# A two-layer pooling and attention trunk in fp32: one PSUM pool, the norm's matmul inside the first up product, attention's end and the last down products in another order

## The chip, the cores and the metric

The kernel runs on one core of a Trainium2 chip. The metric is device time in microseconds (us) of one execution; the time of a kernel is the median over its runs. PE is the matrix engine, DVE the vector engine, ACT the scalar engine, SP the engine whose queue issues most of the DMAs.

## The reference

One sequence of 512 tokens of width 1024 gets 16 learned tokens in front (528 in all) and goes through two residual layers. Layer 0 mixes tokens by causal pooling over windows of 2, 4, 8 and 16, layer 1 by stick-breaking attention with 16 heads of 64. A SwiGLU feed-forward of hidden width 2816 follows each, and a last RMSNorm. The 16 tokens are dropped from the output. All is float32.

```python
h = h + mixer(rmsnorm(h, g1))
h = h + (silu(rmsnorm(h, g2) @ w_gate) * (rmsnorm(h, g2) @ w_up)) @ w_down
...
z = einsum('bqhd,bkhd->bhqk', q, k) * HEAD_DIM ** -0.5
log_keep = where(mask, log_sigmoid(-z), 0.0)
later = cumsum(log_keep, axis=3, reverse=True) - log_keep
a = where(mask, exp(log_sigmoid(z) + later), 0.0)
```

## The kernel before

**Numbers.** Each fp32 operand is split into a high part (a rounding cast on ACT, `wsplit` L92 for weights) and a low part (a subtraction on DVE, L97). Each product is three matmuls, high by high, high by low, low by high (`mm3`, L102 to L108). Activations lie transposed, features on the 128 partitions and tokens along the row: `hT[c]` is chunk c of 8.

**Norms.** `Norm.chunk(c)` (L148) makes from a finished chunk the high part `uh` (ACT, L152), the low part `ul` (DVE, L153) and the square (ACT, L157), and adds squares up on DVE (L161, the last by `add_eps`, L128). `norm_bcast` (L165) sums over partitions with a matmul against ones (L173), and `rstd_of` (L132) makes the scale. The products run on the unscaled `uh` and `ul`, and the scale is multiplied in when a product is evicted.

**Feed-forward** (`ffn`, L271). The hidden width is 22 blocks f of 128. Blocks 0 to 2 are `plain` (L353): 8 chunks of gate and of up products into `pp`, evicted with the norm's scale (L364), silu (L366), product. From block 3 on a block is `strassen` (L392): 7 products of half size in place of 8, over the operands `xh`, `xl` that `operands` (L373) makes once per layer from the scaled activations, chunk pairs m and m + 4 for m = 0 to 3: DVE scales (L381) and makes differences (L387), ACT casts (L389), DVE subtracts (L390). Products go to PSUM tiles `pa`, `pb`, `pc`; ACT copies sums out (`keep`, L412), DVE and ACT form silu and the hidden block (L429 to L436), and `split_hid` splits it into `hh` and `hl` (L349, L350). The down products of a round of blocks (`ROUNDS`, four blocks each after the first two) run beside the next round's gate and up products. In layer 0 these are transposed (`down`, L295, evicted into `hT` at L304). In layer 1 they are by tokens (`down_n`, L320): t is a block of 128 tokens, e a half of the features, and `pd5_te` below is such a product of the last round. At the layer's end the last round runs over c (L462) or over t and e (L468).

**Attention.** The 16 heads are taken as 8 pairs p. `proj(p)` gives the steps of q, k and v (`half`, L503, with products `pj`). `Scores` makes the scores of a pair in three groups of key columns (`z7_832` and `z7_416` are groups of pair 7), sigmoids on ACT (L576), a scan along the row on DVE (L581) and the weights (L583). `turned` (L590) transposes a head's weights on PE (L594, L607), and ACT and DVE split them (L612 to L619); `attend` (L623) multiplies with the values into `po`; `finish` splits a pair's output into `os`. `wo(p0, p1)` (L647) gives the 8 steps of the output projection for pairs p0 to p1 − 1; `pw5_c` is chunk c of the last one, for pairs 5 to 7. The loop at L693 sets by hand what stands between: `fill` holds steps that go before, between and behind the score groups of the next pair.

**What sets the order.** Each engine works through its queue in order. A scheduler places the instructions when the program is built; `issue_after` pins one behind another. PSUM has 8 banks of 512 columns. Four phases use them in turn, each with a pool of its own: `ps0` (8 single banks) for the start, `ps1` (6 and 2) for layer 0's feed-forward, `ps2` (4 single, 2 double) for attention, `ps3` (6 and 2) for layer 1's.

**Last norm.** `square` (L738) sums squares along a row of 512 or 256 features, `store` (L744) scales a token block's two halves (L748 on ACT, L749 on DVE) and stores each with one DMA (L751).

## Time and profile before

| what | value |
|---|---|
| runs | 1058.43, 1060.87, 1235.87 us |
| median | 1060.87 us |
| the profiled execution | 1062.8 us |
| its span on the core | 1061.0 us |
| mean granted PE clock | 0.985 |
| PE, DVE, ACT busy | 96%, 81%, 52% |
| DMA | 95.73 MB, 90 GB/s |

The profile shows one execution. A timeline row has start, length, engine, line, operation, output and inputs, sizes; in brackets stands how long the engine was idle before it and what it waited for. A row of waits sums such idle time by what was waited for. A row of windows gives the busy time in a stretch. Matmul rows overlap: the distance from start to start is what one costs PE.

### The profile page before, as it was taken

The page shows a single profiled execution, that of the slowest core. Times are in us where ns is not written, and L with a number is a line of the kernel's source. Part 1 is how long each engine was busy: PE and PEld are TensorE (multiplying, and loading weights), DVE is VectorE, ACT ScalarE, POOL GpSimd, SP SyncE. Part 2 cuts the span into 40 slices and gives each one's busy share as a digit, 9 for nine tenths or more (in the row PEclk, how much of TensorE's full clock was granted, in tenths as well). Part 3 has the DMA queues.
Part 4 walks back from the last instruction along what each step waited for, and adds up shares of the span by engine and source line. Part 5 has one row for each costly group of instructions (what it writes and reads, how often), then busy time and mean ns, then how long its engine had stood idle before and what let it go on. Part 6 is the DMA issues. An engine that isn't in the chain of part 4 may idle for free.

```text
span 1061.0 us, 18586 instructions
## 1 busy us (share of the span) xinstructions
PE 1023.1 (96%) x7302; PEld 949.3 (89%) x7302; DVE 856.6 (81%) x1529; ACT 556.9 (52%) x1131; POOL 6.2 (1%) x16
## 2 busy tenths in 40 slices
PE   8998999999999999999999998989999999999997
PEld 6997999999999998998888886867899999999985
DVE  7899987888878777678888987779977877788755
ACT  7555645454444455455555454555655444455544
POOL 1000000000000010000000000000000000000000
PEclk9999999999999999999999998989999999999999
DMA  9212323333333332211111211211223223333302
GB/s 351 72 51 69 128 94 100 101 100 100 100 100 100 99 120 82 78 40 61 40 51 37 69 58 66 80 62 58 100 100 115 84 100 99 100 100 120 109 31 80
DMA packets 43112, 95.73 MB, mean 90 GB/s; under 512 B 3328, under 2 KB 20096, under 8 KB 43024
## 3 DMA queue, kind: packets, MB, share of 16 engines
q1 hardware_dynamic: 42272, 93.40, 26.2%
q8 instruction: 57, 0.93, 0.3%
q10 hardware_dynamic: 752, 1.14, 0.3%
q14 instruction: 31, 0.25, 0.1%
HBM read 92.43 MB, written 2.10 MB: 89 GB/s over the span
## 4 chain that ended last, share of the span: by engine, by line
PE 78%; DVE 17%; issue 2%; ACT 1%; DMA 1%; SPq 0%; ACTq 0%; DVEq 0%
PE pb L106 15%; PE pd L106 11%; PE pd L331 11%; PE pa L106 10%; PE pc L106 10%; PE pj L106 9%; PE pp L106 4%; DVE kp L581 2%; PE pw L106 2%; PE z L567 2%; DVE xl L390 1%; DVE a L619 1%; PE t L594 1%; DVE t L387 1%; DVE sg L583 1%
## 5 line engine op out<-in xcount | busy, mean ns | idle before, releaser
L304 DVE TENSOR_TENSOR h<-pd,h 128x264 f32<-128x264 f32 x96 | 40.9, 427 | 14.0 <-PE pd L106 14.0
L92 ACT CAST ws_3h<-rgate 128x512 fp32r<-128x512 f32 x38 | 23.6, 620 | 53.3 <-PE pb L106 47.8
L581 DVE TENSOR_TENSOR_SCAN kp<-kp,estrip 128x1344 f32<-128x1344 f32 x16 | 47.3, 2954 | 3.8 <-ACT kp L576 3.4
L92 ACT CAST ws_4h<-s 128x512 fp32r<-128x512 f32 x38 | 23.6, 621 | 46.6 <-PE pa L106 27.7
L92 ACT CAST ws_5h<-s 128x512 fp32r<-128x512 f32 x38 | 23.6, 621 | 45.8 <-PE pb L106 34.7
L433 DVE TENSOR_TENSOR u<-pb,m 128x264 f32<-128x264 f32 (+1 forms) x38 | 16.3, 428 | 38.6 <-PE pb L106 38.6
L106 PE MATMUL pa<-xl,ws_0h 128*128 128x264 f32 (+1 forms) x152 | 43.3, 285 | 3.1 <-DVE xl L390 3.0
L106 PE MATMUL pb<-xl,ws_1h 128*128 128x264 f32 (+1 forms) x152 | 43.3, 285 | 1.0 <-DVE xl L390 1.0
L106 PE MATMUL pc<-xl,ws_2h 128*128 128x264 f32 (+1 forms) x152 | 43.1, 283 | 0.9 <-DVE xl L390 0.9
L106 PE MATMUL pb<-xh,ws_1h 128*128 128x264 f32 (+1 forms) x152 | 43.6, 287 | 0.2 <-ACT xh L389 0.2
L106 PE MATMUL pa<-xh,ws_3h 128*128 128x264 f32 (+1 forms) x152 | 43.6, 287 | 0.0
L106 PE MATMUL pa<-xl,ws_3h 128*128 128x264 f32 (+1 forms) x152 | 43.5, 286 | 0.0
L106 PE MATMUL pa<-xh,ws_3l 128*128 128x264 f32 (+1 forms) x152 | 43.3, 285 | 0.0
L106 PE MATMUL pc<-xh,ws_2l 128*128 128x264 f32 (+1 forms) x152 | 43.2, 284 | 0.0
L106 PE MATMUL pa<-xh,ws_0h 128*128 128x264 f32 (+1 forms) x152 | 43.1, 284 | 0.0
L106 PE MATMUL pb<-xh,ws_6l 128*128 128x264 f32 (+1 forms) x152 | 43.0, 283 | 0.0
L106 PE MATMUL pa<-xh,ws_0l 128*128 128x264 f32 (+1 forms) x152 | 43.0, 283 | 0.0
L106 PE MATMUL pb<-xh,ws_4l 128*128 128x264 f32 (+1 forms) x152 | 43.0, 283 | 0.0
L106 PE MATMUL pc<-xl,ws_5h 128*128 128x264 f32 (+1 forms) x152 | 42.9, 283 | 0.0
L106 PE MATMUL pb<-xh,ws_1l 128*128 128x264 f32 (+1 forms) x152 | 42.9, 283 | 0.0
L106 PE MATMUL pb<-xl,ws_4h 128*128 128x264 f32 (+1 forms) x152 | 42.9, 282 | 0.0
L106 PE MATMUL pc<-xh,ws_5h 128*128 128x264 f32 (+1 forms) x152 | 42.9, 282 | 0.0
(1179 smaller groups left out, 4110.9 us busy)
## 6 DMA issues: line engine op xcount, KB each, us to landing
rgate<-in_ffn_w_gate_dram SPq DMA_DIRECT2D x44, 512.0 KB, 3.5
rup<-in_ffn_w_up_dram SPq DMA_DIRECT2D x44, 512.0 KB, 3.5
rd<-in_ffn_w_down_dram SPq DMA_DIRECT2D x42, 512.0 KB, 3.6
rq<-in_sb_w_qkv_dram SPq DMA_DIRECT2D x8, 512.0 KB, 3.5
rk<-in_sb_w_qkv_dram SPq DMA_DIRECT2D x8, 512.0 KB, 3.4
rv<-in_sb_w_qkv_dram SPq DMA_DIRECT2D x8, 512.0 KB, 3.4
rwo<-in_sb_w_o_dram SPq DMA_DIRECT2D x8, 384.0 KB, 3.0
h<-in_x_t_dram SPq DMA_DIRECT2D x8, 264.0 KB, 6.9
```

What stands on the lines that cost most here:

```text
L92: nc.scalar.copy(hi, v[:, j:j + w])
L106: last = nc.tensor.matmul(o, lhsT=w, rhs=xx[:, sl], start=start and i == 0, stop=stop and i == 2, skip_group_check=more)
L304: nc.vector.tensor_tensor(out=hv, in0=pd, in1=hv, op=ALU.add)
L331: nc.tensor.matmul(pd, lhsT=hid[j][x_][:, ts], rhs=w_[:, sl], start=r > 0 and i + j == 0, stop=j == len(hid) - 1 and i == 2, skip_group_ch ...
L387: nc.vector.tensor_tensor(out=o, in0=a, in1=b, op=ALU.subtract)
L390: nc.vector.tensor_tensor(out=xl[i][:, m, :], in0=o, in1=f32(xh[i][:, m, :]), op=ALU.subtract)
L433: tt(out=u[:, a], in0=pb, in1=m1, op=ALU.add)
L567: nc.tensor.matmul(tz[:, hd, c:c + k1 - k0], lhsT=qq[hs, i * P:(i + 1) * P], rhs=kk[hs, k0:k1], start=j == 0 and c == 0, stop=False, skip_ ...
L581: nc.vector.tensor_tensor_scan(kp[:, hd, ::-1], kp[:, hd, ::-1], estrip[:, ::-1], 1.0, op0=ALU.mult, op1=ALU.max)
L583: return nc.vector.tensor_tensor(out=sg[:, hd, 0:STRIP - 1], in0=sg[:, hd, 0:STRIP - 1], in1=kp[:, hd, 1:STRIP], op=ALU.mult).ins
L594: nc.tensor.transpose(o, sg[:, c0:c0 + n], ident)
L619: nc.vector.scalar_tensor_tensor(a0[r, i], f32(a0h[r]), lo_rows[r], p2[r, 256:384], op0=ALU.mult, op1=ALU.add)
```

## The change

**PSUM.** The four phases become one pool for the whole program: two double banks (tag `two`) and two single tags `c` and `d` of two banks each. `ps` hands out single tiles of the start and of attention in turn from these. In a Strassen block `pa` and `pb` become the halves of one two-bank tile `pab`, and the copies are made into halves of two tiles.

**Norm and operands.** The matmul of the feed-forward's norm, which stood behind the first gate product, is placed inside the first up product behind chunk `FB` = 4, and the evictions of both products stand behind it. The low halves of the weights of blocks 1 and 2 are pinned behind the norm's last sum or behind its scale. `operands` makes two chunks at once, in two passes of twice the width. `plain` and `strassen` write the silu in place.

**Attention.** `queued` pins a row of steps on PE one behind the other. Pair 7's `fill` moves: no step ahead of the first two score groups, one between, three behind. The last output projection is cut in `begun` (pairs 5 and 6) and `ended` (pair 7), and chunk c + 1 is begun before chunk c is ended.

**The end.** The last round of `down_n` is pinned in the order of t and e. The last token block is scaled and stored in pieces of 256.

```diff
+    psum = ctx.enter_context(tc.tile_pool(name="psum", bufs=1, space=bass.MemoryType.PSUM))
...
+        if tag == "any":
+            if i % 8 in (0, 1, 4, 5):
+                if i % 2 == 0:
+                    turn["tile"] = ps(name, "two", 2)
+                return turn["tile"][:, i % 2]
+            tag = "cd"[i % 2]
+        if tag == "one":
+            tag = "cd"[i % 2]
...
+                        if i == 1 and k == FB and not fst:
+                            with tc.issue_after(last):
+                                fst.extend((norm_bcast([acc], f"fb{layer}", "d"), last_rstd[0]))
+                            mark = last_bcast[0]
...
-                for m in range(4):
+                for m in (0, 2):
...
-                        xn.append(t)
-                    b11, b12, b21, b22 = [t[:, s] for t in xn for s in halves]
+                        xn.append(t)
+                    b11, b12, b21, b22 = [t[:, :, s] for t in xn for s in halves]
...
-                pa, pb, pc = [ps(f"p{i}{f}", "w")[:, :n] for i in "abc"]
+                pab = ps(f"pab{f}", "two", 2)
+                pa, pb, pc = pab[:, 0, :n], pab[:, 1, :n], ps(f"pc{f}", "c")[:, :n]
...
-                    down_n(r, t, e, prev, ws[e], "dw"[e], sl)
+                    with tc.issue_after(mark) if mark else nullcontext():
+                        mark = down_n(r, t, e, prev, ws[e], "dc"[e], sl)
...
-                fill = w[0:1], w[1:2], w[2:4]
+                fill = [], w[0:1], w[1:4]
...
-        for c, st in enumerate(wo(5, NP)):
-            st()
+        queued(lambda: begun(0))
+        for c in range(KC):
+            queued(*([lambda: begun(c + 1)] if c + 1 < KC else []), lambda: ended(c))
...
+            w = 512 if t < 3 else 256
+            cuts = [slice(o, o + w) for o in range(0, 512, w)]
```

Three places of PE's queue, before and after. A row has the line, the operation, the output, the stationary and moving operand by name and number, and the size; a wait for another engine stands in brackets.

*Layer 0's last down product (`pd5_7`) and attention's first product (`pj0_00`, over `anuh` and `anul`, the norm's parts by chunk), up to the norm's matmul (`abp0`). Before:*

```order
L106 MATMUL pd5_7_5452<-hh21_5083,wd0_5_7l0_5435 128x264
L106 MATMUL pj0_00_5504<-anuh0_5188,wq0h0_5495 128x512 [waits DVE_49,Activation_49]
L106 MATMUL pj0_00_5504<-anul0_5189,wq0h0_5495 128x512
L106 MATMUL pj0_00_5504<-anuh0_5188,wq0l0_5496 128x512
...
L106 MATMUL pj0_00_5504<-anuh7_5466,wq0h4_5499 128x512 [waits Activation_49]
L106 MATMUL pj0_00_5504<-anul7_5467,wq0h4_5499 128x512 [waits DVE_49]
L106 MATMUL pj0_00_5504<-anuh7_5466,wq0l4_5500 128x512
L173 MATMUL abp0_5529<-ansq0_5192,ones_62 128x264 [waits DVE_49]
```

*After:*

```order
L125 MATMUL pd5_7_5309<-hh21_4940,wd0_5_7l0_5292 128x264
L125 MATMUL pj0_00_5357<-anuh6_5284,wq0h4_5352 128x512 [waits Activation_49]
L125 MATMUL pj0_00_5357<-anul6_5285,wq0h4_5352 128x512 [waits DVE_49]
L125 MATMUL pj0_00_5357<-anuh6_5284,wq0l4_5353 128x512
L125 MATMUL pj0_00_5357<-anuh7_5323,wq0h4_5352 128x512 [waits Activation_49]
L125 MATMUL pj0_00_5357<-anul7_5324,wq0h4_5352 128x512 [waits DVE_49]
L125 MATMUL pj0_00_5357<-anuh7_5323,wq0l4_5353 128x512
L192 MATMUL abp0_5382<-ansq0_5049,ones_65 128x264 [waits DVE_49]
```

The 24 matmuls of `pj0_00` stood together behind the last down product; now those of chunks 0 to 5 stand among the down products, and six are left.

*The end of attention: the last output projection (`pw5_c`, over `os5` to `os7`) and the first gate product of layer 1 (`pp0`, over `f1uh`, `f1ul`). Before:*

```order
L106 MATMUL pw5_7_8528<-os7h_8359,wo5_7h0_8524 128x512
L106 MATMUL pw5_7_8528<-os7l_8360,wo5_7h0_8524 128x512
L106 MATMUL pw5_7_8528<-os7h_8359,wo5_7l0_8525 128x512
L106 MATMUL pp0_8591<-f1uh0_8380,wgate0h0_8570 128x512 [waits DVE_49,Activation_49]
L106 MATMUL pp0_8591<-f1ul0_8381,wgate0h0_8570 128x512
L106 MATMUL pp0_8591<-f1uh0_8380,wgate0l0_8571 128x512
L106 MATMUL pp0_8591<-f1uh1_8401,wgate0h0_8570 128x512 [waits Activation_49]
```

*After:*

```order
L125 MATMUL pp0_8439<-f1uh0_8244,wgate0h0_8419 128x512 [waits Activation_49]
...
L125 MATMUL pp0_8439<-f1uh1_8267,wgate0h0_8419 128x512 [waits Activation_49]
...
L125 MATMUL pp0_8439<-f1uh2_8289,wgate0h0_8419 128x512 [waits Activation_49]
L125 MATMUL pw5_7_8370<-os5h_7771,wo5_7h0_8366 128x512 [waits DVE_49]
...
L125 MATMUL pw5_7_8370<-os7h_8212,wo5_7h0_8366 128x512
L125 MATMUL pw5_7_8370<-os7l_8213,wo5_7h0_8366 128x512
L125 MATMUL pw5_7_8370<-os7h_8212,wo5_7l0_8367 128x512
L125 MATMUL pp0_8439<-f1ul2_8290,wgate0h0_8419 128x512 [waits DVE_49]
```

The gate product began behind all of `pw5`; now its first two chunks and part of the third stand ahead of the end of `pw5_7`, with `pw5_5` and `pw5_6` between them.

*The last Strassen product (`pb21`, after the change the second half of `pab21`) and the last round's down products. Before:*

```order
L106 MATMUL pb21_12400<-xh6_8560,ws21_6l0_12396 128x256
...
L331 MATMUL pd5_01_12572<-wd1_20_1h0_12546,hh20_12279 128x512 [waits Activation_49]
...
L331 MATMUL pd5_11_12616<-wd1_18_1h0_12536,hh18_11903 128x512
...
L331 MATMUL pd5_21_12660<-wd1_18_1h0_12536,hh18_11903 128x512
...
L331 MATMUL pd5_31_12704<-wd1_18_1h0_12536,hh18_11903 128x256
...
L331 MATMUL pd5_00_12554<-wd1_20_0h1_12530,hh21_12505 128x512 [waits Activation_49]
...
L331 MATMUL pd5_00_12554<-wd1_20_0h1_12530,hl21_12506 128x512 [waits DVE_49]
```

*After:*

```order
L125 MATMUL pab21_12123<-xh6_8409,ws21_6l0_12120 128x256
L351 MATMUL pd5_00_12274<-wd1_20_0h1_12250,hh21_12225 128x512 [waits Activation_49]
L351 MATMUL pd5_00_12274<-wd1_20_0h1_12250,hl21_12226 128x512 [waits DVE_49]
L351 MATMUL pd5_00_12274<-wd1_20_0l1_12251,hh21_12225 128x512
L351 MATMUL pd5_01_12292<-wd1_18_1h0_12256,hh18_11635 128x512
L351 MATMUL pd5_01_12292<-wd1_18_1h0_12256,hl18_11636 128x512
```

Before, 28 matmuls on blocks 18 to 20 stood between the last Strassen matmul and the first use of `hh21`; now that use follows at once.

More of the change, by code (lines that the diff above doesn't have):

```diff
@@ L31 @@
 PLAIN = 3
+FB = 4
 NW = 8
@@ L61, in blk, with ps_pair @@
         return main.tile([P, n], dt, tag="blk", name=name, bufs=NBLK)
-    @contextmanager
-    def phase(name, **bufs):
-        with tc.tile_pool(name=name, bufs=1, space=bass.MemoryType.PSUM) as pool:
-            psum["pool"], psum["bufs"] = pool, bufs
-            yield
-    def ps(name, tag, banks=1):
-        shape = [P, 512] if banks == 1 else [P, banks, 512]
-        return psum["pool"].tile(shape, F32, tag=tag, name=name, bufs=psum["bufs"][tag])
+    psum = ctx.enter_context(tc.tile_pool(name="psum", bufs=1, space=bass.MemoryType.PSUM))
+    turn = {"one": 0, "any": 0, "pair": 0}
+    def ps(name, tag, banks=1):
+        i = turn.get(tag, 0)
+        turn[tag] = i + 1
+        if tag == "any":
[6 more added lines that the diff above has]
+            tag = "cd"[i % 2]
+        shape = [P, 512] if banks == 1 else [P, banks, 512]
+        return psum.tile(shape, F32, tag=tag, name=name, bufs=2)
+    def ps_pair(name):
+        i = turn["pair"]
+        turn["pair"] = i + 1
+        if i % 3 == 2:
+            return [ps(f"{name}{j}", "c") for j in range(2)]
+        pt = ps(name, "two", 2)
+        return [pt[:, 0], pt[:, 1]]
     def wraw(src, name):
@@ L126, in add_eps @@
     def add_eps(out, sq, acc):
[L128 to L130 removed]
+        return nc.vector.scalar_tensor_tensor(out, sq, D * EPS / P, acc, op0=ALU.add, op1=ALU.add).ins
+    last_rstd, last_bcast = [], []
     def rstd_of(parts, r, t):
@@ L172, in norm_bcast @@
             for i, acc in enumerate(accs):
-                nc.tensor.matmul(p, lhsT=ones, rhs=acc[:, o:o + h], start=i == 0, stop=i == len(accs) - 1)
+                last_bcast[:] = [nc.tensor.matmul(p, lhsT=ones, rhs=acc[:, o:o + h], start=i == 0,
+                                                  stop=i == len(accs) - 1).ins]
             parts.append((p, slice(o, o + h)))
@@ L179, in trunk @@
     norm = Norm(16, "f0")
-    with tc.tile_pool(name="start", bufs=1) as sp, phase("ps0", one=8):
+    with tc.tile_pool(name="start", bufs=1) as sp:
         nc.scalar.activation(sp.tile([P, 1], F32, name="table"), ones[:, 0:1], AF.Abs_reciprocal_sqrt)
@@ L330, in down_n @@
                 for i, (x_, w_) in enumerate(((0, wh), (1, wh), (0, wl))):
-                    nc.tensor.matmul(pd, lhsT=hid[j][x_][:, ts], rhs=w_[:, sl], start=r > 0 and i + j == 0,
-                                     stop=j == len(hid) - 1 and i == 2, skip_group_check=r == 0)
+                    last = nc.tensor.matmul(pd, lhsT=hid[j][x_][:, ts], rhs=w_[:, sl], start=r > 0 and i + j == 0,
+                                            stop=j == len(hid) - 1 and i == 2, skip_group_check=r == 0)
             hv = hn[4 * e + t][:, sl]
@@ L388, in operands @@
                     for i, o in enumerate((b11, t2, t1, b21, t3, b22, t4)):
-                        nc.scalar.copy(xh[i][:, m, :], o)
-                        nc.vector.tensor_tensor(out=xl[i][:, m, :], in0=o, in1=f32(xh[i][:, m, :]), op=ALU.subtract)
+                        hi, lo = xh[i][:, m:m + 2, :], xl[i][:, m:m + 2, :]
+                        nc.scalar.copy(hi, o)
+                        nc.vector.tensor_tensor(out=lo, in0=o, in1=f32(hi), op=ALU.subtract)
             def strassen(f):
@@ L480, in before_attention @@
         return norms[0].chunk
-    with phase("ps1", w=6, d=2):
-        ffn(0, 16, norm, before_attention)
-    with tc.tile_pool(name="att", bufs=1) as ap, phase("ps2", one=4, two=2):
+    ffn(0, 16, norm, before_attention)
+    with tc.tile_pool(name="att", bufs=1) as ap:
         uh, ul, acc = norms[0].uh, norms[0].ul, norms[0].acc
@@ L588, in both, with queue, queued @@
                     self.weights(1)
+        pos = []
+        def queue():
+            return tc.issue_after(pos[0]) if pos else nullcontext()
+        def queued(*steps):
+            for st in steps:
+                with queue():
+                    pos[:] = [st()]
         def turned(p, hd, sg):
@@ L668, in begin @@
             sc = Scores(p, got["q"], got["k"])
-            mark = None
-            for st in before:
-                mark = st()
-            with tc.issue_after(mark) if mark else nullcontext():
-                sc.group(0)
-                mark = sc.group(1)
-            for st in between:
-                with tc.issue_after(mark):
-                    mark = st()
-            with tc.issue_after(mark):
-                sc.group(2)
+            queued(*before, lambda: (sc.group(0), sc.group(1))[1], *between, lambda: sc.group(2))
             sc.both()
@@ L686, in trunk @@
         sg = begin(0, got, [], steps[3:4])
-        steps[4]()
+        queued(steps[4])
         values()
         nxt, steps, values = proj(1)
-        for st in steps[:3]:
-            st()
+        queued(*steps[:3])
         early, w = wo(0, 2), wo(2, 5)
```

131 lines of the change are left out of this document (76 added, 55 removed).

## The prediction

> **What bounds the kernel now.** I read the page's busy shares and the shares of the chain first.
>
> ```profile
> PE 1023.1 (96%) x7302; PEld 949.3 (89%) x7302; DVE 856.6 (81%) x1529; ACT 556.9 (52%) x1131; POOL 6.2 (1%) x16
> PE 78%; DVE 17%; issue 2%; ACT 1%; DMA 1%; SPq 0%; ACTq 0%; DVEq 0%
> ```
>
> TensorE is busy for 1023.1 of 1061.0 us; VectorE at 81% is second, and it takes over for 17% of the chain. Where it does so is not in an average, so I cut the span into stages. Each row below is a stretch, its length, then busy time with count of PE, weight loads, DVE, ACT and POOL, then granted clock, DMA share and GB/s.
>
> ```profile
> 76.00:98.00 22.00, 17.55 (x113) 15.43 (x112) 22.00 (x56) 11.31 (x29) 0.00 (x0) 0.92 0.14 51
> 98.00:390.00 292.00, 292.00 (x2400) 292.00 (x2399) 237.45 (x447) 148.15 (x301) 3.27 (x10) 1.00 0.32 105
> 700.00:760.00 60.00, 57.42 (x303) 48.81 (x302) 53.05 (x109) 33.87 (x72) 0.00 (x0) 0.96 0.18 62
> 760.00:1030.00 270.00, 270.00 (x1888) 251.91 (x1888) 211.21 (x375) 138.82 (x284) 0.00 (x0) 1.00 0.30 98
> ```
>
> In the two long feed-forward stretches PE has no gap in 562 us, and nothing that only reorders work can gain there. From 76 to 98 DVE has no gap and PE idles 4.45 us: the activations' Strassen operands are made there, and from 700 to 760 for the second layer. What a reordering can win is in the waits of PE (from whom, total, times, longest):
>
> ```profile
> PE pp L106 <- DVE h L660: 4.1, 1, 4.1
> PE t L594 <- DVE sg L583: 3.6, 1, 3.6
> PE pa L106 <- DVE xl L390: 3.0, 3, 2.1
> PE pb L106 <- DVE xl L390: 1.0, 1, 1.0
> PE pc L106 <- DVE xl L390: 0.9, 1, 0.9
> PE z L567 <- DVE a161l L616: 0.6, 1, 0.6
> ```
>
> **A second price stands behind a wait: the granted clock.** Here the stretches are cut where the clock records change; after the busy time of PE with its count comes the clock.
>
> ```profile
> 38.86:42.27 3.41, 3.21 (x14) 0.50 0.43 156
> ...
> 86.65:90.06 3.41, 3.16 (x13) 0.50 0.00 0
> ...
> 421.16:424.57 3.41, 1.79 (x14) 1.00 0.13 35
> 424.57:427.98 3.41, 3.41 (x23) 0.50 0.31 124
> ...
> 653.26:656.67 3.41, 0.60 (x4) 1.00 0.00 0
> 656.67:663.50 6.83, 6.05 (x20) 0.50 0.22 77
> 690.81:694.22 3.41, 0.20 (x1) 1.00 0.45 150
> 694.22:701.05 6.83, 5.89 (x14) 0.50 0.22 79
> 738.59:742.00 3.41, 2.16 (x12) 1.00 0.00 0
> 742.01:745.42 3.41, 3.41 (x23) 1.00 0.02 5
> 745.42:748.83 3.41, 2.35 (x12) 1.00 0.00 0
> 748.84:752.25 3.41, 3.41 (x17) 0.50 0.43 154
> ```
>
> A stretch of 3.41 us in which PE was busy for 1.79 or less is followed by half rate for 3.41 or 6.83 us; after 2.16 it stayed full once, after 2.35 it fell once. Half rate is real time:
>
> ```profile
> 661.32 0.63 PE L106 MATMUL pw<-os3l,wo_4h 128*128 128x512 f32 x1
> 661.75 0.63 PE L106 MATMUL pw<-os3h,wo_4l 128*128 128x512 f32 x1
> ...
> 1041.40 0.39 PE L331 MATMUL pd<-wd_0h,hh 128*128 128x512 f32 x1
> 1041.63 0.40 PE L331 MATMUL pd<-wd_1h,hh 128*128 128x512 f32 x1
> ```
>
> 512 columns start 0.43 us apart in the first pair, 0.23 in the second. The six half-rate rows hold 25.1 us of PE work, so about 12.6 us is lost to them. I charge 1.7 us (half of 3.41) for each new stretch, times the chance that a wait falls so that it empties one.
>
> The Trainium skill, "TensorE: Matmul & The Clock Gate", Part 1, has the same window (3413 ns, free-running) but says that the clock turns cold after at least one idle window. The trace agrees on the window and not on the condition: the fall at 424.57 follows a window that was busy for 1.79 us. That condition as the Trainium skill states it would lead to the third rival's time.
>
> **The change, place by place** (+ is slower). Times are worked out on the profiled execution, 1062.8 us, which is 1.9 above the median.
>
> *Feed-forward steady state: 0.* One pair of PSUM banks now serves two products, so the copy of m1 holds the first product of `pb` in the same tile, and the silu of `pa` waits for `pb`'s end. In PE's order products of `pc` and down products worth at least 2 us stand between in the steady state; a copy out of PSUM takes about 0.4 (the 264-wide eviction below is 0.43). Price if that cover is gone: the second rival.
>
> *Start of layer 0: +0.5 (−1.5 to +2.5).* The norm's matmul stands inside the first up product, some 1.2 us earlier. The operands come in two passes of two chunks instead of four, so the first product gets its first operand's two chunks together, and its third and fourth wait for a whole second pass.
>
> ```profile
> L304 DVE TENSOR_TENSOR h<-pd,h 128x264 f32<-128x264 f32 x96 | 40.9, 427 | 14.0 <-PE pd L106 14.0
> ```
> ```profile
> 1037.40 0.69 DVE L350 TENSOR_TENSOR hl<-u,hh 128x512 fp32r<-128x512 f32 x1
> ```
>
> Two 264-wide DVE operations take 0.85, one twice as wide 0.69: between nothing and 0.16 is saved on each of 22 pairs; since operations overlap by some 0.07 to 0.1 at their ends I take 0.07, or 1.6. Walking the queues, PE stalls about 9 us in place of the 4.9 of the three `xl` rows, but reaches this place 2.4 earlier: 9 − 4.9 − 2.4 − 1.6 ≈ 0; I leave 0.5 for the later operands.
>
> *Layer 0's end into attention: +3.2 (+1.6 to +4).*
>
> ```profile
> 408.83 0.47 PE L106 MATMUL pj<-anuh,wq0h 128*128 128x512 f32 x1 [0.69 <-ACT wq1h L92]
> ...
> 414.47 1.05 PE L173 MATMUL abp<-ansq,ones 128*128 128x264 f32 x4
> ```
> ```profile
> 411.18 0.70 DVE L128 SCALAR_TENSOR_TENSOR ansq<-ansq,ansq 128x528 f32<-128x528 f32 x1
> ```
>
> The last down product ends at 408.83 − 0.69 = 408.14. The chain from it (eviction of h7, high and low half, square, sum) ends at 411.88, 3.74 later. Before, 24 matmuls of `pj0_00` covered all of it, up to the norm's matmul at 414.47. Now 18 of them stand among the down products, each behind its chunk, and 6 are left: 6 × 0.23 = 1.4. So 2.35 stands bare where 0.69 did: +1.7. One more down product waits for the eviction before it, +0.3. The stall is broken by single matmuls; I give it 7 chances in 10 of a half-rate stretch, +1.2.
>
> *Pairs 0 to 4: 0; pairs 5 and 6: +0.3 (0 to +0.9)*, since two `wo` steps now stand before the next transposes, whose inputs are ready, and so delay ACT's and DVE's work behind these.
>
> *Pair 7: −0.9 (−2.5 to +0.5).* `fill` gives no step ahead of the first two score groups; 9 matmuls (2.1 us) leave the place before `z7_832`. That group's wait for `a161l` grows from 0.6 by 2.1. In return the third group stands ahead of three steps, 27 matmuls (6.2), and `po61` (1.5) covers the scan and what follows it:
>
> ```profile
> 651.83 2.96 DVE L581 TENSOR_TENSOR_SCAN kp<-kp,estrip 128x1344 f32<-128x1344 f32 x1 [1.64 <-ACT kp L576]
> ...
> 655.76 1.55 DVE L583 TENSOR_TENSOR sg<-sg,kp 128x1343 f32<-128x1343 f32 x1
> ```
>
> 2.96 + 1.55 plus a wait is under 7.7, so the 3.6 us gap goes, with its half-rate stretch (6.05/2 = 3.0). Evictions now queue behind the second scan, about +2.0 in three waits. 2.1 − 3.6 + 2.0 − 3.0 = −2.5; the new 2.7 us wait costs a stretch of its own, +1.7 at most: −0.9.
>
> *Attention's end into layer 1: −3.9 (−6.5 to −1).* Matmuls of pair 7's last products and of the first gate product alternate, each behind its chunk. The 4.15 idle and 5.89/2 = 2.95 of half rate go: −7.1. But DVE then makes the operands in about 38 us of its own, before and after, from the norm's scale to the last `xl` (from 700 to 760 it is busy for 53.05 of 60). The scale comes only 5.7 earlier, and PE arrives with more to wait for: +2.4, and +0.8 as half a chance of a further stretch.
>
> *The tail: +4.3 (+1.5 to +7).* The last products are pinned token by token.
>
> ```profile
> 1030.90 0.42 ACT L432 ACTIVATE sg<-g 128x256 f32<-128x256 f32 x1
> ...
> 1035.18 0.28 PE L106 MATMUL pb<-xh,ws_6l 128*128 128x256 f32 x1
> ...
> 1036.75 0.62 ACT L349 CAST hh<-u 128x512 fp32r<-128x512 f32 x1 [0.70 <-DVE u L436]
> ```
>
> From 1035.30, when PE was free, to 1041.40, when the first product took `hh` of block 21, PE had 28 matmuls on other blocks; `hh` was ready at 1037.37, `hl` at 1038.09. Now the first product behind the last Strassen matmul needs `hh`. The silu (0.42) reads the same PSUM tile and stands ahead: `hh` at 1037.8, a bare wait of 2.5; one matmul; `hl` at 1038.5, another 0.5. In front of that the last Strassen product waits for the copy of `m67`, about 1.0. A half-rate stretch after it is nearly certain, +1.7. At the very end there is a gain:
>
> ```profile
> 1052.78 0.28 PE L331 MATMUL pd<-wd_1l,hh 128*128 128x256 f32 x1
> ...
> 1056.57 0.72 ACT L748 ACTIVATE hn<-fss 128x512 f32<-128x512 f32 x1 [0.47 <-DVE fss L139]
> ```
>
> The last scaled piece is ready 4.23 after the last matmul's end. The third and the fourth block of tokens no longer share DVE's queue there, and the pieces are 256 wide (0.42 for 0.72, but two of them): 2.85 by the same operations, −1.4. It has 2 stores more, whose issue lies beside other work. 1.0 + 3.0 + 1.7 − 1.4 = 4.3.
>
> Weight loads and their DMAs move with their steps on SP's queue; at 51 to 105 GB/s in these stretches I charge nothing, and up to 0.5 if a moved one were late, inside the ranges.
>
> **Sum.** 0.5 + 3.2 + 0.3 − 0.9 − 3.9 + 4.3 = +3.5: 1066.3 for an execution like the profiled one, 1060.87 + 3.5 = **1064.4** for the median. The places' ends do not all come together; the forecast's own range is 1055 to 1075.
>
> **Rivals.**
> *Only the gaps close.* The waits of 4.1, 3.6 and 0.7 go with the half-rate stretches at 656.67 and 694.22 (6.0), the stores give 1.4, and what I count as bare is covered by work that I placed wrongly: −15.8, **1045**. For it: these gaps are the three that the edits sit on. Against: PE's queue is in order, and in the tail nothing stands between.
> *The shared PSUM tile holds PE in the steady state.* Each of 38 Strassen blocks waits for m1's copy, 0.4 and a handoff of 0.2: +23, **1084**, slower than before. It decides when less than 0.6 us of other products stands between `pa`'s last and `pb`'s first; I count at least 2.
> *Waits without a drop of the clock.* If only a nearly empty window (0.60 and 0.20 of 3.41 in the rows) were followed by half rate, the new waits, broken or under 3 us, would cost themselves alone: 1.2 + 1.7 + 0.8 + 1.7 = 5.4 less, **1059**. Against it stand the falls at 424.57 and 748.84. The Trainium skill's condition ("TensorE: Matmul & The Clock Gate", Part 1) would give this time.
> *More opens.* Tail, operands of both layers and layer 0's end at the top of their ranges: +3.5 + 2.7 + 2.0 + 2.9 + 0.8 = +12, **1073**.
>
> **Chances.** Forecast 0.55, gaps alone 0.18, shared tile 0.05, no drop 0.12, more opens 0.10. The range of 1048 to 1075 leaves out the shared tile and a good half of the first rival. A measurement of this kernel can tell 2%, that is 1039.7 or 1082.1: faster 0.05 (the far side of the first rival), slower 0.04, same 0.91.
>
> **What would show it.** Right: no wait of PE at the first `pp` product behind attention nor at pair 7's transposes; new waits at `abp`, at `z7_832` and of 2.5 us at the first `pd5_00` product with `hh` of block 21, each followed by clock 0.50; the last store's source ready about 2.9 us after the last matmul. Wrong: PE under 292 in 292 in the steady state; no wait in the tail; or clock 1.00 behind waits of 2 us and more.

## The result: 1073.41 us, slower by 1.3%

| what | before | after |
|---|---|---|
| median | 1060.77 us (4 runs) | 1073.41 us (4 runs, 1072.82 to 1075.66) |
| ratio, 95% interval | | 1.0131 [1.0106, 1.0155] |
| the profiled execution | 1062.8 us | 1073.62 us |
| its span | 1061.0 us | 1071.5 us |
| mean granted PE clock | 0.985 | 0.979 |

One run of the kernel before, 1235.87 us, was disturbed and is left out of the ratio. The changed kernel is 12.6 us slower by the medians and 10.5 us by the two spans. The forecast was 1064.4 with a range to 1075. The time lies in the range, but it is the time of the rival "more opens", 1073, and not that of the forecast.

**The page after**, busy shares:

```profile
PE 1029.0 (96%) x7302; PEld 951.3 (89%) x7302; DVE 858.5 (80%) x1486; ACT 551.3 (51%) x1104; POOL 7.2 (1%) x16
```

The number of matmuls is the same. PE is busy 5.9 us longer with them, most of it half rate: the half-rate rows below hold 34.2 us of PE work, those of the kernel before 25.1, and half of the difference is 4.5. The other 4.6 of the 10.5 us is idle time. These are PE's longest waits (from whom, total, times, longest):

```profile
PE pab L125 <- DVE xl L425: 4.8, 2, 2.5
PE pool L268 <- DVE pl L275: 3.3, 2, 2.7
PE pd L351 <- ACT hh L370: 3.1, 1, 3.1
PE z L601 <- DVE a161l L662: 2.7, 1, 2.7
PE pd L351 <- DVE hl L371: 2.6, 1, 2.6
```

The waits of 4.1 (`pp` behind attention's end) and 3.6 (pair 7's transposes) are gone. In their place stand waits for `a161l` and for `hh` of block 21, and smaller ones for `anul` at layer 0's end and for `mb` in the tail (rows below), at the places that the prediction named. The wait for `pl`, in the start's pooling stage, and the one for `hl`, at 739.43 among layer 1's operands, it did not name.

**A long stretch and layer 1's operands after** (stretch, length, busy time with count of PE, weight loads, DVE, ACT, POOL; clock, DMA share, GB/s):

```profile
98.00:390.00 292.00, 292.00 (x2398) 291.81 (x2396) 235.80 (x446) 141.70 (x297) 0.00 (x0) 1.00 0.31 104
706.00:710.28 4.28, 4.28 (x20) 3.54 (x19) 0.05 (x1) 2.58 (x4) 0.00 (x0) 1.00 0.68 235
710.28:750.94 40.66, 34.50 (x150) 27.82 (x150) 40.59 (x67) 20.76 (x35) 0.00 (x0) 0.87 0.19 63
```

In the steady state PE has no gap, before and after, so the shared PSUM tile holds nothing up. In the last row DVE is the engine without a gap, and PE idles for 6 us; in the row above it, DVE stands idle for 4.23 of 4.28 us. That pair of rows carries the miss of the prediction at attention's end.

**The clock after** (stretch, length, PE busy with count, clock, DMA share, GB/s), each half-rate stretch behind the window ahead of it:

```profile
17.02:20.43 3.41, 0.70 (x6) 1.00 1.06 386
20.43:23.84 3.41, 3.41 (x18) 0.50 1.04 412
78.45:81.86 3.41, 1.58 (x11) 1.00 0.21 85
81.87:92.10 10.23, 7.26 (x28) 0.50 0.12 43
416.37:419.78 3.41, 1.91 (x6) 1.00 0.03 12
419.79:423.19 3.40, 3.40 (x12) 0.50 0.30 94
645.06:648.47 3.41, 0.73 (x7) 1.00 0.28 113
648.48:655.29 6.81, 6.81 (x31) 0.50 0.01 2
737.22:740.63 3.41, 1.19 (x4) 1.00 0.00 0
740.64:750.87 10.23, 6.93 (x23) 0.50 0.14 40
1037.60:1041.00 3.40, 0.75 (x7) 1.00 0.00 0
1041.01:1047.83 6.82, 6.39 (x14) 0.50 0.01 2
```

Each of the waits above has half rate behind it or around it, and four of the six stretches last 6.8 or 10.2 us rather than 3.41.

**Where the time went.** The table follows PE through its queue by the start of the same matmul, or of the matmul with the same number, in both profiled executions.

| point | before | after | difference | added since |
|---|---|---|---|---|
| first gate product of block 0, layer 0 | 39.06 | 40.35 | +1.3 | +1.3 |
| 1500th matmul, mid feed-forward of layer 0 | 204.97 | 207.81 | +2.8 | +1.5 |
| first key product of pair 2 | 456.12 | 461.40 | +5.3 | +2.5 |
| last key product of pair 7 | 614.04 | 619.41 | +5.4 | +0.1 |
| last projection's first matmul (`os5`) | 674.12 | 680.45 | +6.3 | +1.0 |
| first up product of block 1, layer 1 | 715.53 | 715.63 | +0.1 | −6.2 |
| 6300th matmul, mid feed-forward of layer 1 | 903.11 | 907.36 | +4.3 | +4.2 |
| last matmul | 1052.78 | 1064.65 | +11.9 | +7.6 |
| end of the span | 1061.0 | 1071.5 | +10.5 | −1.4 |

Each column is one execution, and which windows half rate falls into differs between executions of the same instructions. The run `before_fill` below has those of the kernel before up to pair 7, but reaches the same first gate product later, with the same wait in front of it (the kernel before, then `before_fill`):

```profile
39.06 0.78 PE L106 MATMUL pp<-f0uh,wgate0h 128*128 128x264 f32 x2 [2.19 <-DVE h L266]
```
```profile
40.77 0.48 PE L106 MATMUL pp<-f0uh,wgate0h 128*128 128x264 f32 x2 [2.19 <-DVE h L266]
```

So a difference at one place of up to 1.7 us, the price of one stretch of 3.41, is not shown to come from the change.

### The profile page after: what moved, and what is told of

Read it like the earlier page. It is cut to its first block, busy times and chain, and to the rows that moved or that the text cites. A ratio compares the mean times of both kernels' runs of the same rounds, so it can differ in the third digit from the quotient of the medians.

```text
span 1071.5 us, 18530 instructions
## 1 busy us (share of the span) xinstructions
PE 1029.0 (96%) x7302; PEld 951.3 (89%) x7302; DVE 858.5 (80%) x1486; ACT 551.3 (51%) x1104; POOL 7.2 (1%) x16
## 4 chain that ended last, share of the span: by engine, by line
PE 77%; DVE 17%; ACT 3%; issue 2%; DMA 1%; SPq 0%; DVEq 0%; ACTq 0%
PE pab L125 25%; PE pd L351 12%; PE pd L125 11%; PE pc L125 10%; PE pj L125 9%; DVE kp L615 2%; PE z L601 2%; PE pw L125 2%; PE pp L125 1%; DVE a L665 1%; DVE xl L425 1%; DVE sg L617 1%; PE mix L125 1%; DVE xn L415 1%; DVE of L682 1%
## 5 line engine op out<-in xcount | busy, mean ns | idle before, releaser
L125 PE MATMUL pab<-xl,ws_0h 128*128 128x264 f32 (+1 forms) x152 | 43.7, 288 | 4.8 <-DVE xl L425 4.8
L125 PE MATMUL pc<-xh,ws_2h 128*128 128x264 f32 (+1 forms) x152 | 43.5, 286 | 1.1 <-DVE u L397 1.1
L125 PE MATMUL pab<-xh,ws_0h 128*128 128x264 f32 (+1 forms) x152 | 43.4, 285 | 1.0 <-ACT xh L424 1.0
L125 PE MATMUL pab<-xh,ws_6h 128*128 128x264 f32 (+1 forms) x152 | 43.0, 283 | 0.9 <-ACT mb L456 0.9
L125 PE MATMUL pab<-xh,ws_0l 128*128 128x264 f32 (+1 forms) x152 | 43.7, 287 | 0.0
L125 PE MATMUL pab<-xh,ws_6l 128*128 128x264 f32 (+1 forms) x152 | 43.1, 283 | 0.0
L125 PE MATMUL pab<-xh,ws_4l 128*128 128x264 f32 (+1 forms) x152 | 43.0, 283 | 0.0
L125 PE MATMUL pab<-xl,ws_1h 128*128 128x264 f32 (+1 forms) x152 | 43.0, 283 | 0.0
L125 PE MATMUL pab<-xh,ws_1h 128*128 128x264 f32 (+1 forms) x152 | 43.0, 283 | 0.0
L125 PE MATMUL pab<-xl,ws_3h 128*128 128x264 f32 (+1 forms) x152 | 43.0, 283 | 0.0
```

What stands on the lines that cost most here:

```text
L125: last = nc.tensor.matmul(o, lhsT=w, rhs=xx[:, sl], start=start and i == 0, stop=stop and i == 2, skip_group_check=more)
```

## The experiments

The theory at this point: the loss sits in three places where the change bares a chain on DVE and ACT (layer 0's end, pair 7, the tail), each with half rate behind it, and in layer 1's operands, where PE's earlier arrival meets a scale that comes later than forecast. The rivals were that the pool's banks and not the pins bare the tail, and that the clock alone, not the chains, makes the loss. Four runs changed the kernels as given. All ratios are to the kernel before, timed in the same rounds (its medians there: 1059.54 to 1060.76); changes that leave part of the loss in place are compared by their medians.

**The tail without its pins** (`tail_free`).

```diff
-                    with tc.issue_after(mark) if mark else nullcontext():
-                        mark = down_n(r, t, e, prev, ws[e], "dc"[e], sl)
+                    down_n(r, t, e, prev, ws[e], "dc"[e], sl)
```

> The changed kernel with one thing undone: the last round's down products are no longer pinned by tokens. Theory 1 (the pins took the cover away): the cover of about 6 us comes back, the wait of 3.1 us at hh of block 21 and the half rate behind it (6.83 us, 3.4 lost) go, about -6, near 1067. Theory 2 (the cover is lost by the number of free PSUM banks: one pool leaves four banks to these products, and their work on blocks 18 to 20 is put ahead of the last Strassen product): 2 matmuls stand in the gap, the wait stays at about 2.6 and the clock still falls; only the copy's wait of 0.9 and the second wait at hl go, -1 to -2, near 1072.

Measured: 1069.82, ratio 1.0097 [1.0083, 1.0111], 3.6 better than the changed kernel: neither 6 nor 1 to 2. PE's timeline behind the last Strassen product (start, length, then the operation; a wait in brackets), and the clock there:

```profile
1043.78 0.63 PE L351 MATMUL pd<-wd_1l,hh 128*128 128x512 f32 x2
1047.03 0.50 PE L351 MATMUL pd<-wd_0h,hh 128*128 128x512 f32 x1 [2.62 <-ACT hh L370]
```

```profile
1042.21:1045.62 3.41, 2.20 (x16) 1.00 0.00 0
1045.62:1049.03 3.41, 2.00 (x9) 1.00 0.00 0
```

Without the pins the scheduler again puts work on blocks 18 to 20 early, but ahead of the last Strassen product: only four bank-sized tiles are left for the last products in the one pool, so it starts four pairs, and two matmuls stand in the gap. The wait stays at 2.62. What is gained is the wait for `m67` and the half rate: the idle time is split over two windows, each busy for 2.00 or more, and the clock did not fall. So the pins alone do not bare the tail; the scheduler's order in the one pool does it without them.

**The tail with cover put in by hand** (`tail_cover`). The products over blocks 18 to 20 of the first two token blocks are pinned behind the last Strassen product; block 21's follow in the order of t and e.

```diff
+            for t, e in ((0, 0), (0, 1), (1, 0), (1, 1)):
+                with tc.issue_after(mark or lastmm[0]) if t + e else nullcontext():
+                    mark, half[t, e] = down_n(r, t, e, prev, ws[e], "dc"[e], part=slice(0, 3))
```

> The changed kernel with the last down products still pinned, but in another order: the products of blocks 18 to 20 of the first four (token, half) pairs stand behind the last Strassen product, ahead of the first use of block 21. Same work, 19 matmuls (4.4 us) in the gap. Both theories of the tail: the wait at hh of 3.1 us, the copy's 0.9 and the half rate behind (3.4) go: -6 to -7, near 1067. If the tail's loss were something else than the bare chain (the pieces of the stores, the shared tile), it would stay above 1071.

Measured: 1067.13, ratio 1.0071 [1.0055, 1.0087], 6.3 better than the changed kernel. The timeline, up to the first product with block 21:

```profile
1038.63 0.39 PE L351 MATMUL pd<-wd_1l,hh 128*128 128x512 f32 x1
...
1043.03 0.39 PE L351 MATMUL pd<-wd_0h,hh 128*128 128x512 f32 x1
```

```profile
750.50:1061.00 310.50, 306.61 (x2114) 1.00 0.30 95
```

PE goes on for 4.4 us on the other blocks, no row of that stretch has a wait, and the clock is 1.00 from there to the end. The last matmul comes 7.8 us earlier than in the changed kernel. The stall in the tail with what follows it cost these 6.3 us, shown by taking it away. The same four tiles serve here, so it is the order and not the number of tiles that bares the chain.

**The tail's wait filled with work nobody reads** (`tail_fill`): 13 matmuls more, into an unread PSUM tile, in the place of the wait for `hh`. The chain to `hh` stays as it is.

```diff
+                    spare = ps("spare", "two", 2)[:, 0]
+                    with tc.issue_after(lastmm[0]):
+                        for _ in range(NFILL):
+                            last = nc.tensor.matmul(spare, lhsT=hid[0][0][:, ts], rhs=w[0][0][:, sl], start=True,
+                                                    stop=True)
```

> The changed kernel with 13 extra matmuls (3.0 us; their sums go to a PSUM bank that nobody reads) between the last Strassen product and the first use of block 21's hh. The chain behind the wait is not shorter. Theory: the clock falls because PE stood idle for most of a 3.41 us window, so with PE kept busy it stays at 1.00 from 1041 to 1048: -3.4, near 1070. Rival: the clock falls for another reason (time, load, the end of a phase): no change, 1073, and 0.50 still in those windows.

Measured: 1071.82, ratio 1.0117 [1.0104, 1.0131]: 1.6 better by the medians, with intervals that overlap. In the trace:

```profile
1039.04 3.15 PE L356 MATMUL spare<-wd_0h,hh 128*128 128x512 f32 x13
1042.28 0.50 PE L361 MATMUL pd<-wd_0h,hh 128*128 128x512 f32 x1
```

```profile
1038.91:1042.33 3.42, 3.33 (x17) 1.00 0.00 0
```

The clock stays at 1.00, in the next window too. The way from the last `ws_4l` product to the span's end is 33.4 us against 36.0: 2.6 of the tail's loss is clock, and the rest bare chain. The clock's part is read from the trace; the medians alone do not resolve it.

**The same in the kernel before** (`before_fill`): 14 spare matmuls in front of pair 7's transposes and 16 behind the last projection, where it had 3.6 and 4.1 us of waiting and two half-rate stretches.

```diff
+            if p == NP - 1:
+                spare = ps("spare", "two", 2)[:, 0]
+                with tc.issue_after(lastpo[0]):
+                    for _ in range(14):
+                        nc.tensor.matmul(spare, lhsT=osp[0][0][:, 0:P], rhs=osp[0][0], start=True, stop=True)
```

> The kernel before with 14 extra matmuls in the 3.6 us gap ahead of pair 7's transposes and 16 in the 4.15 us gap at the end of attention (their sums go to PSUM that nobody reads). Theory: the two half-rate stretches of 6.83 us behind these gaps go, 6.05/2 + 5.89/2 = 6.0 less, near 1055; the waits themselves stay. Rival (the clock falls for another reason): 1061 or, if the extra work delays the next product, above.

Measured: 1058.22, ratio 0.9993 [0.9985, 1.0002], where the price of half the busy time gives 6. Both stretches are at full clock:

```profile
658.28:661.69 3.41, 3.41 (x17) 1.00 0.00 0
...
695.83:699.24 3.41, 3.41 (x16) 1.00 0.15 61
```

By the trace the stage at attention's end is 2.8 shorter, close to the priced 2.95, but the one at pair 7 only 1.1, against 3.0. There PE, now faster, waits for DVE instead:

```profile
664.79 0.38 PE L633 MATMUL po<-a270l,vv 128*128 128x256 f32 x1 [0.25 <-DVE a270l L616]
666.16 0.50 PE L633 MATMUL po<-a,vv 128*128 128x512 f32 x1 [0.98 <-DVE a L619]
```

The kernel before has no such waits there. Two things follow: half rate costs its full half only where PE sets the end; and even the 3.9 us that the trace shows is not in the medians (−1.3). The profiled execution of the kernel before is longer than most: it lies 1.9 above its median, and its mean clock of 0.985 is below that of all 17 runs timed beside `before_fill` (0.986 to 0.990). So a usual run has less half rate to lose. Its stretch at 424.57, for one, is absent in `before_fill`, where nothing was edited up to there.

The next four stand on `tail_cover` and undo or change one part each, so their base is 1067.13.

**The norm's matmul of layer 1 behind the first chunk** (`c_fb`), in place of chunk 4; layer 0 is left.

```diff
-FB = 4
+FB = (4, 0)
```

> tail_cover with one more thing moved: in layer 1 the norm's matmul stands behind chunk 0 of the first up product instead of chunk 4 (layer 0 keeps 4). In the changed kernel's trace the sum of squares is ready at 703.6, the matmul starts at 707.6, and DVE stands idle for 4.2 us until the scale. Theory (DVE bounds the stretch from the scale to the last operand, about 40 us): the scale comes 3 us earlier, PE's waits at the operands shrink by as much, -3, near 1064. Rival (PE bounds the stretch, or the table load and the evictions behind set it): 0 to -1, 1066 to 1067.

Measured: 1064.10, ratio 1.0041 [1.0025, 1.0057], −3.0. DVE's timeline of the changed kernel, from the last square's sum to the scale, then PE's row for the norm's matmul, and DVE's in this run:

```profile
702.93 0.70 DVE L147 SCALAR_TENSOR_TENSOR f1sq<-f1sq,f1sq 128x528 f32<-128x528 f32 x1
...
710.28 0.71 DVE L155 TENSOR_TENSOR fb1t<-fb1r 128x528 f32<-128x528 f32 x1 [4.24 <-ACT fb1r L154]
```
```profile
707.60 1.05 PE L192 MATMUL fb1p<-f1sq,ones 128*128 128x264 f32 x4
```
```profile
701.12 0.70 DVE L147 SCALAR_TENSOR_TENSOR f1sq<-f1sq,f1sq 128x528 f32<-128x528 f32 x1
...
705.69 0.71 DVE L155 TENSOR_TENSOR fb1t<-fb1r 128x528 f32<-128x528 f32 x1 [1.46 <-ACT fb1r L154]
```

In the changed kernel the sum of squares is ready at 703.63 and the norm's matmul, behind four chunks of the up product, starts at 707.60; DVE idles for 4.24. In this run sum to scale takes 4.6 us instead of 7.4. By the traces the operands' stage gets 2.2 shorter. Another 1.5 comes from pair 7, where the half-rate stretch is 3.41 instead of 6.83 long; nothing of the edit is there, so that part is not the edit's.

**Operands in four passes again, in both layers** (`c_ops`).

```diff
-                for m in (0, 2):
+                for m in range(4):
```

> tail_cover with the operands made in four passes of one chunk again. Theory 1 (two passes make PE wait: first products need the second pass early): PE's waits at both layers' operands fall, -1.5 in layer 0 and -2 in layer 1, near 1063.5. Theory 2 (DVE bounds these stretches, and the twice as wide operations save it time): 22 more DVE operations per layer at 0.07 each, +1.6 per layer at most, 1067 to 1070.

Measured: 1065.96, ratio 1.0052 [1.0036, 1.0068], −1.2 with overlapping intervals. By stages it is two results: up to the twelfth Strassen block of layer 0 +2.1, in layer 1's feed-forward −2.1. In layer 0 the waits for `xl` (the longest 2.2 us between 70 and 125 us in the changed kernel) go and another takes their place; PE's longest there in this run:

```profile
PE pd L125 <- DVE h L324: 4.6, 4, 2.2
```

The evictions of layer 0's first down products stand in DVE's queue among the operands. Neither expectation holds in both layers: four passes gain nothing in layer 0 and are better in layer 1. That they cost 2.1 in layer 0 is not shown. Here the half-rate stretch is 13.65 us long, 6.83 in the base; `c_wo` below, with two passes as in the base, has one of 13.65 too and is 1.6 later than the base at the 1500th matmul.

**Attention's first product whole behind the last down product** (`c_pj`).

```diff
-        for st in steps[:3]:
+        with tc.issue_after(lastdown[0]):
+            steps[0]()
+        for st in steps[1:3]:
             st()
```

> tail_cover with attention's first product pinned behind layer 0's last down product again, 24 matmuls in one piece. Theory: the waits of 0.6 and 0.9 at the last two chunks and of 0.5 between the down products go, -2.0, and so does the half-rate stretch behind them where the window falls so, up to -1.7: -2 to -3.5, near 1064.5. Rival (the loss there comes from the pool, not from the order): no change.

Measured: 1062.52, ratio 1.0023 [1.0011, 1.0036], −4.6, more than expected. PE's rows of the changed kernel, then PE's window of this run around the same place:

```profile
417.34 0.50 PE L125 MATMUL pj<-anul,wq0h 128*128 128x512 f32 x1 [0.64 <-DVE anul L172]
...
419.24 0.50 PE L125 MATMUL pj<-anul,wq0h 128*128 128x512 f32 x1 [0.86 <-DVE anul L172]
```
```profile
405.00:430.00 25.00, 23.37 (x168) 1.00 0.26 86
```

The two waits and the half rate at 419.79 are gone. The stage is 3.6 shorter by the trace, and pair 7, where nothing was edited, again 1.5, with a half-rate stretch of 3.41. The profiled execution, at 1059.78, is among the fastest of this kernel's 12 runs (1059.71 to 1064.60), so the trace shows more gain (spans 1063.8 and 1057.8) than the medians do.

**Pair 7's steps between the score groups as before** (`c_p7`).

```diff
-                fill = [], w[0:1], w[1:4]
+                fill = w[0:1], w[1:2], w[2:4]
```

> tail_cover with pair 7's fill as before: one projection step ahead of the first score groups, one between, two behind. Theory: the wait of 2.7 us for a161l falls to 0.6 and the half-rate stretch behind it goes (6.83 us, 3.4); the cover of the scan shrinks by 9 matmuls to 5.7 us, so about 1 us of wait comes back ahead of the transposes: -2 to -4, near 1064. Rival (the wait only moves: the 3.6 us gap of the kernel before comes back whole, with its half rate): 0 to +1.

Measured: 1063.52, ratio 1.0036 [1.0023, 1.0049], −3.6; the stage is 4.05 shorter. The waits at the third score group and at the transposes, after this edit; in the changed kernel the first was 2.67, and the second had gone:

```profile
647.71 0.50 PE L607 MATMUL z<-qk_1h,qk_0h 64*128 64x512 f32 x2 [0.57 <-DVE a161l L668]
...
660.02 0.74 PE L645 MATMUL t<-consts,sg 128*128 128x128 f32 x5 [0.83 <-DVE sg L623]
```
```profile
640.00:676.00 36.00, 32.94 (x199) 1.00 0.22 72
```

The clock is 1.00 throughout. The gap at the transposes is only 0.83 with the old `fill` too (3.6 in the kernel before), so moving `fill` was not needed to close it. What differs in PE's queue is the order that `queued` pins: it has 9 projection matmuls ahead of the third score group and 18 behind it, where the scheduler of the kernel before had put 21 ahead and 6 behind.

**All of it together** (`best`): `tail_cover`, `c_fb`, `c_pj` and `c_p7`, with operands in two passes in layer 0 (`full`) and four in layer 1.

```diff
+                two = full
+                for m in (0, 2) if two else range(4):
```

> tail_cover with what the single runs showed put together: the norm's matmul of layer 1 behind chunk 0, attention's first product in one piece, pair 7's fill as before, operands in two passes in layer 0 and in four in layer 1. If the places are independent, the stage differences add: 1067.1 - 2.2 (scale earlier) - 3.6 (first product) - 4.1 (pair 7) - 2.1 (four passes in layer 1) = 1055, about 4 under the kernel before. If the four passes and the earlier scale give the same time twice (both shorten the wait for DVE's operands), -2 less: 1057.

Measured: 1054.36, ratio 0.9949 [0.9936, 0.9961]: 5.5 faster than the kernel before and 19 faster than the change as made. What is left of PE's longest waits, beside the start's for `pl` (3.4 in two):

```profile
PE pd L345 <- ACT hn L357: 2.8, 1, 2.8
```

In layer 1 the down products of the first round wait for an eviction (0.8 in the changed kernel), probably since PE arrives earlier.

**Weight sums of one block per layer on GpSimd** (`best_pool`), to relieve DVE where it sets the end.

```diff
-                        nc.vector.tensor_tensor(out=o, in0=a, in1=b, op=op)
+                        (nc.gpsimd if f == PLAIN else nc.vector).tensor_tensor(out=o, in0=a, in1=b, op=op)
```

> The kernel best, with the four weight sums of the first Strassen block of each layer on POOL instead of DVE (4 x 0.68 us of DVE less in each layer's stretch of operands; POOL is idle there). Theory (DVE bounds these stretches): PE's waits shrink by up to 2.7 in each layer, -3 to -5 against best. Rival (POOL is so slow, or shares so much with DVE, that the sums come late and hold the first Strassen products): 0 or slower than best.

Measured: 1066.60, ratio 1.0058 [1.0044, 1.0072]: 12.2 slower than `best`. First one of GpSimd's four sums in a layer, for both layers (count, then busy total and mean ns), then DVE's low halves of two weights while it ran, then the same two in `best`:

```profile
L442 POOL TENSOR_TENSOR s<-rgate,rup 128x512 f32<-128x512 f32 x2 | 3.5, 1740 | 0.0
```
```profile
58.55 3.51 DVE L116 TENSOR_TENSOR wup2l<-rup,wup2h 128x512 fp32r<-128x512 f32 x2
```
```profile
57.64 1.29 DVE L116 TENSOR_TENSOR wup2l<-rup,wup2h 128x512 fp32r<-128x512 f32 x2
...
58.85 0.68 DVE L442 TENSOR_TENSOR s<-rup 128x512 f32<-128x512 f32 x1
```

This sum takes 1.74 us on GpSimd, one on DVE 0.68, and DVE's own two operations take 3.51 in place of 1.29 meanwhile. The scheduler also moved work at layer 0's end, with a new half-rate stretch there, so not all of the 12 us comes from the slower sums and DVE operations.

**The last projection in whole chunks again** (`c_wo` on `tail_cover`, `best_wo` on `best`), to see whether the interleaving `begun`/`ended` closed the wait of 4.1 us, or the one pool.

```diff
-        queued(lambda: begun(0))
-        for c in range(KC):
-            queued(*([lambda: begun(c + 1)] if c + 1 < KC else []), lambda: ended(c))
+        wos = wo(5, NP)
+        queued(lambda: (wos[0](), norms[1].chunk(0))[0])
+        for c in range(1, KC):
+            queued(lambda: (wos[c](), norms[1].chunk(c))[0])
```

> tail_cover with attention's last projection in whole chunks again, one after the other as before the change, in the one PSUM pool. Theory 1 (the 4.15 us wait was the border between two PSUM pools: the first gate product waited for the last eviction): without a border the product starts at once behind the last projection and keeps pace with the norm's halves, PE loses at most 1.5, and the stretch behind is bound by DVE from a scale that comes at nearly the same time: 0 to +1.5, 1067 to 1068.5. Theory 2 (the interleaving of the chunks made the gain): the wait of about 4 us and a half-rate stretch come back ahead of the gate product, +4 to +7, 1071 or more.

> The kernel best with attention's last projection in whole chunks again. Theory 1 (the border between pools made the wait): +0 to +1.5, 1054.4 to 1056. Theory 2 (the interleaving made the gain, and only shows where the scale is not late for another reason): +3 to +5, 1057.5 to 1059.5.

Measured: 1067.21, ratio 1.0063 [1.0051, 1.0075], beside 1067.13 for `tail_cover`; and 1055.63, 0.9959 [0.9946, 0.9972], beside 1054.36 for `best`. No difference that can be told. The stage up to the first up product of block 1 is 1.4 longer, and layer 1's operands give 0.95 of it back. The 4.1 us did not return with the whole chunks, so the interleaving did not close it. By elimination it belonged to the border between the pools, where the first product of the next phase took a bank of attention's; no run interleaves with two pools.

## Why the prediction was right in range and wrong in its sum

Point by point, as the sum had it; the sizes are those of the table by places.

**Steady state, forecast 0: right.** PE is busy 292.00 of 292.00.

**Start and operands of layer 0, forecast +0.5: +2.8.** The table puts +1.3 of this before the first gate product, in the pooling stage, which the prediction did not price. There the tiles come in turn from another set of banks, and one matmul waits 2.7 us for `pl`, while the 2.19 in front of the first gate product is gone. But the +1.3 can't be put down to the change: the start has one half-rate stretch of 3.41 in each of three traces, at 38.86 before, behind that product, and at 20.43 after and 19.98 in `before_fill`, ahead of it. Beside `before_fill` the changed kernel reaches the product 0.4 earlier and the 1500th matmul (205.60 there) 2.2 later, so by these traces the loss lies at the operands. Between 70 and 125 PE is idle for 5.6 us, less than the 9 that "Walking the queues, PE stalls about 9 us" gave, but the half-rate stretch there lasts 10.23 us (one of 3.41 before), which was not foreseen. The four-pass run gets nothing of it back, so the two passes are not shown to be the cause.

**Layer 0's end, forecast +3.2: +2.5, right in mechanism, the size in part by luck.** Waits for the eviction's chain, then half rate; `c_pj` takes both away and 3.6 with them. The kernel before had a stretch of its own near there in its profiled execution, at 424.57; beside `before_fill`, which has none, the stage is 3.9 longer.

**Pairs 5 and 6, forecast +0.3: +0.1, right.**

**Pair 7, forecast −0.9: +1.0, wrong sign.** (Its terms add up to −0.8.) The wait for `a161l` was forecast as 0.6 + 2.1 and is 2.67:

```profile
647.90 0.50 PE L601 MATMUL z<-qk_1h,qk_0h 64*128 64x512 f32 x2 [2.67 <-DVE a161l L662]
```

The step that failed is "the new 2.7 us wait costs a stretch of its own, +1.7 at most": the stretch is 6.81 us long with 6.81 of work in it, 3.4 of loss; behind the same wait it was 3.41 long in `c_fb` and `c_pj`. And the 3.0 credited for the old half rate was too much, since `before_fill` gets only 1.1 from it: DVE's `a` is next.

**Attention's end into layer 1, forecast −3.9: −2.1.** The gap closes as forecast: −6.2 up to the up product of block 1, against −7.1. The step that failed is "The scale comes only 5.7 earlier". The operations that end in the scale `fb1r` follow DVE's row at 710.28 in the changed kernel and at 708.29 before:

```profile
708.29 0.71 DVE L136 TENSOR_TENSOR fb1t<-fb1r 128x528 f32<-128x528 f32 x1 [2.30 <-ACT fb1r L135]
```

Counted from the last projection's first matmul (680.45 and 674.12) that is 29.8 us and 34.2, so the scale comes 4.3 earlier. I had moved the norm's matmul forward by the time that PE gained, and not looked at what stands ahead of it in the new order: four chunks of the up product. DVE, which sets the end from there on, stood idle for 4.24 us ahead of it, 2.30 before. So of the 6.2 that PE gained, 4.2 were returned in front of the operands, where it waits and runs at half rate for 10.23 us (3.41 before); the term of +0.8 for a further stretch was too small as well. `c_fb` and `c_ops` recover 2.2 and 2.1 there.

**The tail, forecast +4.3: +7.6 at the last matmul, −1.4 behind it, +6.3 in all.** The chain is the one described, link by link: the wait for `m67` 0.86 (forecast 1.0), for `hh` 3.09 (2.5), and the last store's −1.4 (−1.4). PE's and ACT's rows:

```profile
1036.67 0.39 PE L125 MATMUL pab<-xh,ws_6h 128*128 128x256 f32 x1 [0.86 <-ACT mb L456]
...
1041.44 0.80 PE L351 MATMUL pd<-wd_0h,hh 128*128 128x512 f32 x1 [3.09 <-ACT hh L370]
```
```profile
1038.33 0.62 ACT L111 CAST wd_1h<-rd 128x512 fp32r<-128x512 f32 x1 [1.71 <-PE pab L125]
1038.86 0.38 ACT L462 ACTIVATE sg<-pab 128x256 f32<-128x256 f32 x1
```

Two terms were mis-sized. ACT casts a weight between the products' end and the silu, which puts the silu at 1038.86; its 0.62 is the size by which `hh` is later than priced. And "a half-rate stretch after it is nearly certain, +1.7" was a stretch of 3.41; it lasted 6.82 with 6.39 of work, 3.2 of loss (2.6 by `tail_fill`). The prediction blamed the pins; `tail_free` shows that the cover is gone without them too, by the scheduler's order in the one pool, and `tail_cover` that pins in another order bring it back.

**The clock.** The common error is the price of one stretch. The falls came after windows that were busy for 0.70, 0.73, 0.75, 1.19, 1.58 and 1.91 of 3.41 us, so the rival "waits without a drop" fell with them; the windows of 2.00 and 2.20 in `tail_free` kept full clock. The Trainium skill ("TensorE: Matmul & The Clock Gate", Part 1) asks for at least one idle window; the row of 1.91 shows a fall where PE worked for over half of it. Busy time is not all of it, though: in `before_fill` the window from 37.05 to 40.46, busy for 1.53, was followed by full clock. What was wrong was the length, taken as 3.41 although the prediction's own rows have two of 6.83 behind the waits of 3.6 and 4.1: at layer 0's operands, pair 7, layer 1's operands and in the tail it was 6.8 to 10.2.

**The range** held only because it took in the rival that opens four places at their worst. That its 1073 is the measured time is luck: layer 0's end and attention's end stayed inside their ranges, and pair 7, which it leaves out, gave 1.9 of the miss. What the places have in common is one cause, a chain on DVE or ACT laid bare with half rate behind it, so their terms do not average out as independent ones would.

Open remain what stretches the half rate at layer 0's operands, and how much of a half-rate stretch's length is chance. The pins on the weights of blocks 1 and 2, the silu in place and the stores' pieces were not undone singly either.

## What to carry to other kernels

When work is cut finer and moved forward to fill one gap, list what it covered where it stood: here three of the four moved pieces had been the cover of a chain of 2.5 to 4 us on other engines. Place a matmul that starts a long chain by when its input is ready and by who waits for its result, not by where PE has room: behind four chunks, it left DVE, which set the end there, idle for 4.2 us. Where PE sets the end, price a bare wait of 2.5 us or more with 3.4 to 6.8 us of half rate behind it, 1.7 to 3.4 of loss, and look for independent matmuls to put into it. Before reading a place's gain out of two traces, see whether each is a usual run of its kernel.

## What the hardware showed that was not expected

- Half rate lasted 3.41, 3.40, 6.81, 6.82, 10.23 and 10.23 us in the changed kernel; the two longest are those in which PE also waited inside (7.26 and 6.93 busy of 10.23). That does not fix the length: in `tail_cover` one of 6.83 at 84.93 held only 4.62 of work.
- Whether a wait costs clock depends on how it falls into the windows: 2.62 us split over two windows busy for 2.20 and 2.00 cost none, 2.67 us inside one busy for 0.73 cost 3.4 us, and in `c_fb` and `c_pj` 1.7. So an edit elsewhere can shift a stretch, as in `c_fb` and `c_pj`, where pair 7's got 3.4 us shorter and the stage 1.5.
- Matmuls whose result nobody reads hold the clock as well as others (1.00 through 3.15 us of them).
- An elementwise sum of 128x512 takes 1.53 to 1.74 us on GpSimd and 0.68 on DVE, and two DVE operations beside such sums took 3.51 in place of 1.29.
